# Making the operands of a two-way recurrence in the input projection, by feature block for all tokens

## The chip, the cores and the metric

One core of a Trainium2 chip runs the whole kernel. The metric is the device time of one execution in microseconds; the runs shown below are three of the kernel before the change, and one further execution was profiled.

## What is computed

A diffusion backbone of two layers works on 1024 latent tokens and 256 context tokens of width 1024. In each layer a token mixer is followed by a feed-forward part; one combined projection feeds two groups of heads, a two-way RWKV-7 recurrence (8 heads of 64, in pairs: NP = 4 blocks of 128 features) and attention with latent queries, keys and values (8 heads). Cut to the mixer's recurrence and what it reads:

```python
def rwkv_prepare(z, w0, w_b, a0, a_b, g_b, k_k, k_a):
    r, k, v, w_lo, a_lo, g_lo = jnp.split(z, idx, axis=-1)
    w_log = -softplus(-(w0 + einsum('btdl,dlc->btdc', tanh(w_lo), w_b))) - 0.5
    decay = exp(-exp(w_log))
    a = sigmoid(a0 + einsum('btdl,dlc->btdc', a_lo, a_b))
    g = sigmoid(g_lo) @ g_b
    kk = k * k_k, normalised per head
    k_dir = k[:, :, None, :] * (1.0 + (a - 1.0) * k_a)

def step(s, inp):                     # once per token and direction
    r_t, w_t, k_t, v_t, kk_t, a_t = inp
    sa = einsum('bhvk,bhk->bhv', s, kk_t)
    s = s * w_t - sa * (kk_t * a_t) + v_t k_t^T
    return s, einsum('bhvk,bhk->bhv', s, r_t)

bonus = sum(r * k_dir * r_k, over directions and features) * v
out = (group_norm(y) + bonus) * g
```

z is the projection after a filter of three taps along the tokens. Direction 1 runs through the tokens backwards. Attention (`mla_prepare`, `attend`) normalises its latents, applies the rotary tables to part of the queries and keys, and takes a softmax over all keys.

## The kernel before

Each layer goes through four stages: `in_proj`, `mixer`, `out_proj`, `ffn`. Layer 0's `in_proj` also makes the modulation of both layers from 48 chunks of `w_ada` (`modulation`). A scheduler sets a fixed order of the instructions of each engine ahead of the run; an engine works through its list in order and waits where an operand is missing. All transfers are issued by SP's queue, in order.

**Projection.** The transposed input lies in SBUF as high and low halves (`uh`, `ul`). A column j of 128 features is made by `col(j)`: `split_w` loads the weights and splits them (ACT L264, DVE L266), `project` issues 72 matmuls (L280) for all 1280 tokens, or 48 for the 1024 latents, into one of two PSUM buffers `pj`. `conv` applies the filter (ACT L287, DVE L291 and L294). Small results (sums of squares, means) use two PSUM buffers `sm`; temporaries of 128x1280 have nine buffers. First come the attention's latents, keys and values, then `queries` (the six weights of `w_uq`, rotary products L419 to L424, writes L411 and L426 into `qD`) behind the first key column. The columns follow in this order:

```python
            order = (4, 5, 6, 7, 12, 13, 8, 9, 10, 11, 0, 1, 2, 3, 14)
```

Keys are 4 to 7 (normalised to kk, ss L480), the LoRA inputs 12 and 13, values 8 to 11 (centred per head, mu L469), r 0 to 3, gate 14 (`gates`). r, k, v, kk and centred v are written to DRAM (`rkvD`), the LoRA inputs to `loD`, the gate's product to `gD`.

**Mixer.** It has ten iterations of 128 tokens per direction; direction 0 goes forwards and direction 1 backwards, so iteration i takes two different token groups (`groups`). `mixer` interleaves attention blocks with the two 64-token steps of the recurrence:

```python
            for i in range(10):
                ...
                self.rwkv_seq(l, i, 0)
                self.rwkv_seq(l, i, 1)
                if i < 9:
                    self.rwkv_inv2(l, i + 1)
                ...
                if i < 8:
                    self.rwkv_prep(l, i + 2)
```

`rwkv_prep` loads r, k, v, kk (L668) and the LoRA inputs, makes the LoRA products (L647, tanh L651), the running sums of the decay (scans L676 and L678), their exponentials E and En (L682, L684), and on POOL the products kd, ta, BK and KR (L687 to L713). It transposes v (L721) and copies it into W (L724). Then g = KR against BK (L736), its masks (L739, L742), and the transposes of BK (L746). `rwkv_bonus` (L586 to L600) makes the bonus where the second direction reaches a token group. `rwkv_inv` solves the 64-token block by 62 steps on DVE (L789, L790). `rwkv_seq` (L841 to L890) carries the state. `attn` has scores L939, maximum L940, exponential L952, transposes L971, copies L974 and L976, values L981. `rwkv_out` applies norm, bonus and gate.

Of the kernel before, what the change touches and what calls it, by code (L numbers as in the profile page):

```python
# [19 lines left out]
D = 1024  # L20
# [40 lines left out]
CO_RST = 486  # L61
CO_N = 998


N_EARLY = 7

# [13 lines left out]
class Kern:  # L80
# [8 lines left out]
    def run(self):  # L89
        tc, nc, a = self.tc, self.nc, self.a  # L90
        with ExitStack() as st:
            dp = st.enter_context(tc.tile_pool(name="dram", bufs=1, space=DRAM))
            cp = st.enter_context(tc.tile_pool(name="const", bufs=1, reuse_waits="tile"))
            self.cst = cp.tile([128, CO_RST], F32, name="cst")
            nc.sync.dma_start(out=self.cst, in_=a["consts"][:, 0:CO_RST])
# [5 lines left out]
            self.rkvD = [dp.tile([20, 128, NTOK], F32, name=f"rkvD{l}") for l in range(DEPTH)]  # L101
            self.loD = [dp.tile([3, 128, NTOK], F32, name=f"loD{l}") for l in range(DEPTH)]
# [5 lines left out]
            self.kdD = [dp.tile([NTOK // 128, 128, NP, 128], F32, name=f"kdD{l}") for l in range(DEPTH)]  # L108
            self.gD = [dp.tile([NP, 128, NTOK], F32, name=f"gD{l}") for l in range(DEPTH)]
            self.boD = [dp.tile([NTOK // 64, 128, NP, 64], F32, name=f"boD{l}") for l in range(DEPTH)]  # L110
            self.mixD = [dp.tile([NTOK // 128, 128, 8, 128], F32, name=f"mixD{l}") for l in range(DEPTH)]
            self.pv, self.msc = [], []
# [114 lines left out]
    def first_u(self, p, pp, pj):  # L227
# [3 lines left out]
        def tile(name, n):  # L231
            return p.tile([128, NTOK], F32, name=name, tag="t", bufs=9)[:, :n]

        def load(t):
# [4 lines left out]

        k4 = lambda t: t[:, :1024].rearrange("p (k n) -> p k n", k=4)  # L240
        spare = [lambda tag=f"{nm}{i}": k4(p.tile([128, NTOK], F32R, name="wt", tag=tag).bitcast(F32))
                 for i in range(3) for nm in ("lh", "ll")]
        spare += 5 * [self.mod_tile] + 5 * [lambda: k4(tile("wt", NTOK))]
# [52 lines left out]
    def in_proj(self, l, up):  # L296
# [3 lines left out]
        with ExitStack() as st:  # L300
            wp = st.enter_context(tc.tile_pool(name=f"iw{l}", bufs=3, side="right", reuse_waits="tile"))
            p = st.enter_context(tc.tile_pool(name=f"ip{l}", bufs=1, reuse_waits="tile"))
# [3 lines left out]
            if l == 0:  # L306
                self.alloc_u(up)
                self.mod_setup(st, 2, sm)
                self.first_u(p, sm, pj)
                todo = [(0, ch) for ch in range(8, 24)] + [(1, ch) for ch in range(24)]  # L310
# [91 lines left out]
            def queries():  # L402
# [24 lines left out]

            def gates(o, n):

                nc.scalar.activation(o[:, :n], o[:, :n], AF.Tanh, scale=0.5)  # L430
                nc.gpsimd.tensor_scalar(o[:, :n], o[:, :n], 0.5, 0.5, op0=ALU.mult, op1=ALU.add)
                h, lo = tmp("gh", F32R), tmp("gl", F32R)
                nc.scalar.activation(h[:, :n], o[:, :n], AF.Copy)
                nc.vector.tensor_tensor(lo[:, :n], o[:, :n], h[:, :n], op=ALU.subtract)
                w = self.split_w(a["g_b"][l], 512, wp)
                parts = [[[x[:, so:so + sn] for so, sn in SEGS]] for x in (h, lo)]
                for q in range(NP):
                    ps = pj.tile([128, 1536], F32, name="pj", tag="pj")
                    wq = [[x[:, q * 128:(q + 1) * 128] for x in w[0]]]
                    self.project(ps, wq, *parts, range(3 if need_ctx else 2))  # L440
                    g = tmp("g")
                    nc.scalar.activation(g[:, :n], ps[:, :n], AF.Copy)
                    nc.sync.dma_start(out=self.gD[l][q, :, :n], in_=g[:, :n])


            order = (4, 5, 6, 7, 12, 13, 8, 9, 10, 11, 0, 1, 2, 3, 14)
            for i, j in enumerate(order):
                full = need_ctx or 4 <= j < 14
                n = NTOK if full else NLAT
                ps = col(j, (0, 1, 2) if full else (0, 1))  # L450
                if i == 0:
                    queries()
                for m in todo[len(todo) * i // 15:len(todo) * (i + 1) // 15]:
                    self.modulation(*m)
                o = tmp("o")
                self.conv(o, ps, PV_CONV + 3 * j, pv, full)
                if j == 14:
                    gates(o, n)
                    continue
                if j >= 12:  # L460
                    nc.sync.dma_start(out=self.loD[l][j - 12], in_=o)
                    continue
                nc.sync.dma_start(out=self.rkvD[l][j, :, :n], in_=o[:, :n])
                if j >= 8:

                    oc = tmp("oc")
                    for so, sn in SEGS:
                        mu = sm.tile([128, 512], F32, name="mu", tag="sm")
                        nc.tensor.matmul(mu[:, :sn], self.cst[:, CO_BLK:CO_BLK + 128], o[:, so:so + sn], start=True, stop=True)  # L469
                        nc.vector.scalar_tensor_tensor(oc[:, so:so + sn], mu[:, :sn], -1.0 / 64, o[:, so:so + sn],  # L470
                                                       op0=ALU.mult, op1=ALU.add)
                    nc.sync.dma_start(out=self.rkvD[l][16 + j - 8], in_=oc)
                if 4 <= j < 8:
                    kcol = pv[:, PV_KK + j - 4:PV_KK + j - 3]
                    sq = tmp("sq")
                    nc.scalar.activation(sq, o, AF.Square, scale=kcol)
                    rn = tmp("rn")
                    for so, sn in SEGS:
                        ss = sm.tile([128, 512], F32, name="ss", tag="sm")
                        nc.tensor.matmul(ss[:, :sn], self.cst[:, CO_BLK:CO_BLK + 128], sq[:, so:so + sn], start=True, stop=True)  # L480
                        nc.vector.tensor_scalar(rn[:, so:so + sn], ss[:, :sn], 1e-24, None, op0=ALU.max)
                    nc.scalar.activation(rn, rn, AF.Ln)
                    nc.scalar.activation(rn, rn, AF.Exp, scale=-0.5)
                    nc.vector.scalar_tensor_tensor(rn, o, kcol, rn, op0=ALU.mult, op1=ALU.mult)
                    nc.sync.dma_start(out=self.rkvD[l][12 + j - 4], in_=rn)
# [57 lines left out]
    def rwkv_setup(self, l, st):  # L543
        tc, nc, a = self.tc, self.nc, self.a
# [4 lines left out]
        p = R.pr  # L549
        R.rst = p.tile([128, 512], F32, name="rst")  # L550
        nc.sync.dma_start(out=R.rst, in_=a["consts"][:, CO_RST:CO_N])
        R.eps = R.p.tile([128, 1], F32, name="eps")
        nc.gpsimd.memset(R.eps, GN_EPS)
        R.wb = p.tile([128, 512], F32, name="wb")
        nc.sync.dma_start(out=R.wb, in_=a["w_b"][l])
        R.ab = p.tile([128, 512], F32, name="ab")
        nc.sync.dma_start(out=R.ab, in_=a["a_b"][l])

        R.hb = p.tile([128, 16], F32, name="hb")
        nc.vector.tensor_scalar(R.hb, self.pv[l][:, PV_W0:PV_W0 + 16], 0.5, None, op0=ALU.mult)  # L560
        R.ka = p.tile([128, 8], F32, name="ka")
# [64 lines left out]
    def rwkv_prep(self, l, i):  # L626
# [33 lines left out]
        for d, tg in enumerate(self.groups(i)):  # L660
# [3 lines left out]
            for nm, j in (("r", 0), ("k", 4), ("v", 16), ("kk", 12)):  # L664
                if nm == "r" and not out_y:
                    continue
# [656 lines left out]
```

## Time and profile before

| | us |
|---|---|
| median of three runs (lowest, highest) | 4727.77 (4719.02, 4730.01) |
| the profiled execution: time, span | 4722.71, 4720.9 |
| busy PE, DVE, ACT, POOL in the span | 4203.5, 2814.2, 1779.0, 1081.6 |
| layer 0: projection, mixer, output, feed-forward | 573, 902, 131, 954 |
| layer 1: the same | 416, 874, 143, 727 |

The engines are PE (matmul), PEld (its weight loads), DVE (vector), ACT (scalar), POOL (GpSimd) and SP (whose queue issues the transfers). The first part of the profile gives each engine's busy time in the span; the stages in the last two lines are cut from the trace where one stage's matmuls follow another's. The mean granted clock of PE over the span was 0.922. The profile's wait view names, for each wait, the instruction whose end released it; its groups by line give busy time, the mean of one instruction, and the idle time ahead of them.

### The profile page before, as it was taken

The numbers are of one execution on the slowest core, as the hardware profiler recorded it, in microseconds if no ns is written. First come the engines' busy times: TensorE is split into PE (matmuls) and PEld (weight loads), VectorE is DVE, ScalarE is ACT, GpSimd is POOL, SyncE is SP. The second block draws the span as 40 slices with busy tenths as digits, with TensorE's granted clock in tenths as the row PEclk, the third lists the DMA queues.
The fourth block names the chain that finished last, engine by engine and source line by source line (L and its number), as shares of the span: only waits on it lengthen the run. The fifth ranks groups of instructions, "written<-read, shape, count | busy, mean of one in ns | idle before, by whom it ended". The sixth has DMA issues, their size and how long they took to land. (4 is left out here: it accounts for less than half of the span.)

```text
span 4720.9 us, 73923 instructions
## 1 busy us (share of the span) xinstructions
PE 4203.5 (89%) x29722; PEld 3387.0 (72%) x29722; DVE 2814.2 (60%) x4905; ACT 1779.0 (38%) x3484; POOL 1081.6 (23%) x1126
## 2 busy tenths in 40 slices
PE   8979988887888899999998989788888768999998
PEld 6757666666666788888886868566666656888887
DVE  3233378788885644444546243578888857555556
ACT  3221265554554432222224231555555634222222
POOL 1000054444442400000004000334454434100002
PEclk9999988788888999999998999878888979999999
DMA  4246722222223311111113232311222233211111
GB/s 169 99 151 218 237 65 71 57 70 66 70 64 119 110 45 34 41 39 34 47 34 107 81 106 109 91 47 51 61 69 68 60 118 133 67 50 45 45 52 65
DMA packets 305063, 385.13 MB, mean 82 GB/s; under 512 B 59088, under 2 KB 208016, under 8 KB 304720
## 3 DMA queue, kind: packets, MB, share of 16 engines
q1 hardware_dynamic: 304720, 380.41, 25.5%
q8 instruction: 233, 3.82, 0.3%
q14 instruction: 110, 0.90, 0.1%
HBM read 287.95 MB, written 92.37 MB: 81 GB/s over the span
## 5 line engine op out<-in xcount | busy, mean ns | idle before, releaser
L1133 PE MATMUL up<-u,hi 128*128 128x512 f32 (+1 forms) x3520 | 1012.2, 369 | 2.9 <-ACT hi L1124 2.9
L1133 PEld LDWEIGHTS up<-u,hi 128*128 128x128 f32 x3520 | 643.4, 189 | 118.1 <-ACT hi L1124 3.1
L1133 PE MATMUL up<-u,lo 128*128 128x512 f32 (+1 forms) x1760 | 648.3, 368 | 0.1
L280 PE MATMUL pj<-u,whi 128*128 128x512 f32 (+1 forms) x1888 | 544.4, 374 | 44.7 <-DVE o L294 33.9
L1180 DVE TENSOR_TENSOR acc<-dn,acc 128x512 f32<-128x512 f32 x340 | 233.5, 689 | 432.2 <-PE dn L1174 432.1
L280 PEld LDWEIGHTS pj<-u,whi 128*128 128x128 f32 x1888 | 342.3, 192 | 124.8 <-issue 53.4
L1133 PEld LDWEIGHTS up<-u,lo 128*128 128x128 f32 x1760 | 332.2, 189 | 58.3 <-DVE lo L1126 0.5
L939 PE MATMUL sp<-ka,qa 96*128 96x512 f32 (+1 forms) x1200 | 340.1, 417 | 36.0 <-ACT P L952 33.7
L981 PE MATMUL av<-pT,va 128*64 128x128 f32 x2624 | 253.8, 319 | 120.1 <-DVE pT L976 75.6
L280 PE MATMUL pj<-u,wlo 128*128 128x512 f32 (+1 forms) x944 | 351.8, 373 | 0.0
L1124 ACT ACTIVATE hi<-raw 128x512 fp32r<-128x512 f32 x176 | 110.5, 630 | 566.1 <-PE up L1133 563.1
L1174 PE MATMUL dn<-hi,fh 128*128 128x512 f32 x792 | 311.6, 393 | 8.4 <-DVE acc L1180 4.3
L1174 PE MATMUL dn<-lo,fh 128*128 128x512 f32 x792 | 310.0, 391 | 0.0
L1174 PE MATMUL dn<-hi,fl 128*128 128x512 f32 x792 | 305.9, 390 | 0.0
L981 PEld LDWEIGHTS av<-pT,va 128*64 128x64 f32 x2624 | 163.4, 156 | 190.3 <-DVE pT L976 74.6
L789 DVE TENSOR_TENSOR tmp<-Dt,T 128x126 f32<-128x126 f32 (+22 forms) x620 | 292.6, 472 | 11.6
L939 PEld LDWEIGHTS sp<-ka,qa 96*128 96x128 f32 x1200 | 228.7, 217 | 85.2 <-ACT P L952 42.9
L952 ACT ACTIVATE P<-sp,mx 128x512 f32<-128x512 f32 (+1 forms) x400 | 240.2, 609 | 125.6 <-DVE mx L949 75.2
L790 DVE TENSOR_TENSOR T<-T,tmp 128x126 f32<-128x126 f32 (+22 forms) x620 | 272.4, 439 | 12.0
L264 ACT ACTIVATE whi<-raw 128x512 fp32r<-128x512 f32 (+2 forms) x110 | 66.0, 603 | 545.6 <-PE pj L280 480.9
L940 DVE TENSOR_REDUCE mx<-sp 128x1 f32<-128x512 f32 (+1 forms) x400 | 229.3, 587 | 70.6 <-PE sp L939 68.8
L971 PE MATMUL tp<-cst,P 128*128 128x128 f32 x1312 | 252.7, 320 | 11.2 <-ACT P L952 9.1
(257 smaller groups left out, 7797.0 us busy)
## 6 DMA issues: line engine op xcount, KB each, us to landing
wt<-in_w_ada_dram SPq DMA_DIRECT2D x96, 512.0 KB
raw<-in_w_up_dram SPq DMA_DIRECT2D x176, 256.0 KB
raw<-in_w_down_dram SPq DMA_DIRECT2D x88, 256.0 KB
raw<-in_w_in_dram SPq DMA_DIRECT2D x84, 256.0 KB
rkvD<-o SPq DMA_DIRECT2D x20, 640.0 KB
k<-rkvD SPq DMA_DIRECT2D x40, 256.0 KB
v<-rkvD SPq DMA_DIRECT2D x40, 256.0 KB
kk<-rkvD SPq DMA_DIRECT2D x40, 256.0 KB
```

What stands on the lines that cost most here:

```text
L280: nc.tensor.matmul(ps[:, o:o + n], ww, u[k][s], start=k == 0 and j == 0, stop=k == nk - 1 and j == 2)
L789: eng.tensor_tensor(tv, bc(Dt[:, j + 1:, j:j + 1], [128, r, w]), bc(T[:, j:j + 1, :w], [128, r, w]), op=ALU.mult)
L790: eng.tensor_tensor(T[:, j + 1:, :w], T[:, j + 1:, :w], tv, op=ALU.subtract)
L939: nc.tensor.matmul(sp[:, o - b0:o - b0 + n], q[:, qq, e], A.k[e][:, kk, o:o + n], start=m == 0, stop=m == 2)
L940: nc.vector.tensor_reduce(mx[:, i:i + 1], sp[:, :w], axis=AX.X, op=ALU.min)
L952: nc.scalar.activation(P[:, o:o + w], sp[:, :w], AF.Exp, bias=mn, scale=-1.0, accum_out=mx[:, 4 + i:5 + i])
L971: nc.tensor.transpose(tp[:, b, e], Ps[e][:, o:o + 128], self.ident)
L981: nc.tensor.matmul(av[half[e], 0:128], A.v[:, k0 // 128 + kt, half[e]], pT[:, b, e], start=kt == 0, stop=kt == nkt - 1)
L1124: nc.scalar.activation(hi, raw, AF.Copy)
L1133: nc.tensor.matmul(ps[:, so:so + sn], ww, uu[k][s], start=k == 0 and m == 0, stop=k == 7 and m == 2)
L1174: nc.tensor.matmul(ps, x[:, t * 128:(t + 1) * 128], w, start=m == 0, stop=m == 3 * len(js) - 1)
L1180: nc.vector.tensor_tensor(dst, ps, dst, op=ALU.add)
```

## The change

Making the recurrence's operands moves from `rwkv_prep` to `in_proj`. The LoRA columns 12 and 13 come first and stay in SBUF. Then, for each block q of 128 features and all 1280 tokens: the key column, the value column (with 2 x 10 transposes), the r column, the LoRA products, scans, exponentials, products, and the bonus. The products are on DVE, where most were on POOL. Results go to DRAM, in the direction's own order of tokens, as `vtD`, `kkD`, `bkD` and `boD`; the decay over 64 tokens stays in SBUF (`pc`). The gate column follows, and then, in a new pool of buffers, the attention's latents, keys, values and last its queries. Temporaries have 13 buffers. `rwkv_prep` now loads BK, KR and W, with two buffers for BK, and goes on with g. PE has 22422 instructions for 22484, DVE 4941 for 4907, ACT 2574 for 3086, POOL 539 for 1131, SP 1808 for 1420.

```diff
+                def lora(w, x, bcol, q):
+                    ts = [tmp("lt") for d in range(2)]
+                    for so, sn in SEGS:
+                        ps = [sm.tile([128, 512], F32, name="lo", tag="sm") for d in range(2)]
+                        for d in range(2):
+                            nc.tensor.matmul(ps[d][:, :sn], w[half[d], q * 128:(q + 1) * 128], x[half[d], so:so + sn],
+                                             start=True, stop=True)
+                        for d in range(2):
...
+                            nc.scalar.activation(dst, src[:, ::-1] if d else src, AF.Tanh, bias=hb[:, b:b + 1], scale=0.5)
+                    return ts
...
+                for q in range(NP):
+                    k, kk = key(q)
+                    v = value(q)
+                    r = column(q, need_ctx)
+                    ths, tas = lora(wb, lw, 0, q), lora(ab, la, 8, q)
+                    kds = []
+                    for d in range(2):
+                        th, ta = ths[d], tas[d]
+                        rv = (lambda t: t[:, ::-1]) if d else (lambda t: t)
+                        nc.scalar.activation(th, th, AF.Copy, scale=0.5, bias=0.5)
+                        Ls = tmp("Ls")
+                        for t in (0, NTOK // 2):
+                            nc.vector.tensor_tensor_scan(Ls[:, t:t + NTOK // 2], rst, th[:, t:t + NTOK // 2], 0.0,
+                                                         op0=ALU.mult, op1=ALU.add)
...
+                        nc.scalar.activation(E[:, :, 1:65], chunks(Ls), AF.Exp, scale=-C0)
+                        nc.scalar.activation(Ls, Ls, AF.Exp, scale=C0)
...
+                        nc.vector.tensor_tensor(chunks(o), chunks(rv(kk)), E[:, :, 0:64], op=ALU.mult)
+                        nc.sync.dma_start(out=self.kkD[l][d, 0, q], in_=o)
...
+                        nc.vector.tensor_tensor(chunks(o), chunks(r), Er[:, :nr // 64], op=ALU.mult)
+                        nc.sync.dma_start(out=self.kkD[l][d, 1, q, :, :nr], in_=o)
+                        kd = tmp("kd")
+                        nc.scalar.activation(kd, ta, AF.Identity, scale=ka[:, q:q + 1], bias=ka[:, 4 + q:5 + q])
+                        nc.vector.tensor_tensor(kd, kd, rv(k), op=ALU.mult)
+                        kds.append(kd)
+                        nc.vector.scalar_tensor_tensor(ta, ta, 1.0, rv(kk), op0=ALU.add, op1=ALU.mult)
+                        nc.vector.scalar_tensor_tensor(ta, ta, 0.5, Ls, op0=ALU.mult, op1=ALU.mult)
+                        nc.sync.dma_start(out=self.bkD[l][d, 1, q], in_=ta)
+                        nc.vector.tensor_tensor(Ls, kd, Ls, op=ALU.mult)
+                        nc.sync.dma_start(out=self.bkD[l][d, 0, q], in_=Ls)
+                    kb = tmp("kb")[:, :nr]
+                    nc.vector.tensor_tensor(kb, kds[0][:, :nr], kds[1][:, ::-1][:, :nr], op=ALU.add)
+                    nc.vector.scalar_tensor_tensor(kb, kb, pv[:, PV_RK + q:PV_RK + q + 1], r, op0=ALU.mult, op1=ALU.mult)
+                    bo = tmp("bo")
+                    for so, sn in SEGS[:3 if need_ctx else 2]:
+                        ps = sm.tile([128, 512], F32, name="bop", tag="sm")
+                        nc.tensor.matmul(ps[:, :sn], self.cst[:, CO_BLK:CO_BLK + 128], kb[:, so:so + sn], start=True, stop=True)
+                        nc.vector.tensor_tensor(bo[:, so:so + sn], ps[:, :sn], v[:, so:so + sn], op=ALU.mult)
...
+                o = column(14, need_ctx)
+                gates(o, nr)
...
-            for nm, j in (("r", 0), ("k", 4), ("v", 16), ("kk", 12)):
...
-            nc.scalar.activation(th, th, AF.Copy, scale=0.5, bias=0.5)
...
-                eng.tensor_tensor(BK[he, :, :, kt], self.rev(kd[he], d), nE, op=ALU.mult)
-                eng.tensor_tensor(BK[he, :, :, bt], self.rev(ta[he], d), nE, op=ALU.mult)
...
+            for e in range(2):
                 he = half[e]
...
+                for kind, o in ((0, 64 * (1 - e)), (1, 64 * e)):
+                    for c in range(2):
+                        src = self.bkD[l][d, kind, :, he, s * 128 + c * 64:s * 128 + c * 64 + 64]
+                        nc.sync.dma_start(out=BK[he, :, c, o:o + 64], in_=src.rearrange("q p t -> p q t"))
+                nc.sync.dma_start(out=KR[he, e].rearrange("p q c t -> p q (c t)"),
+                                  in_=self.kkD[l][d, 0, :, he, tok].rearrange("q p t -> p q t"))
             if out_y:
...
+                    nc.sync.dma_start(out=KR[:, 2, :, c], in_=self.kkD[l][d, 1, :, :, b * 64:b * 64 + 64].rearrange("q p t -> p q t"))
...
+                    nc.sync.dma_start(out=Ws[c][half[1 - e], e, d], in_=self.vtD[l][d, s, half[c], :, e * 64:e * 64 + 64])
```

The order in which the scheduler puts this stands below at three places; lines are those of the changed kernel.

PE in the projection of layer 0, from the end of the second block's r column (pj, L282) on; lo is a LoRA product, bop the bonus, ps and pt a modulation chunk:

```order
L282 MATMUL pj<-u_115,wlo 128x256
L384 MATMUL lo<-lw,wb 128x512
L384 MATMUL lo<-lw,wb 128x256 x2
L384 MATMUL lo<-la,ab 128x512 x4
L384 MATMUL lo<-la,ab 128x256 x2
L477 MATMUL bop<-kb,cst 128x512 x2
L477 MATMUL bop<-kb,cst 128x256
L173 MATMUL ps<-wt,sc 32x256 x8
L188 MATMUL pt<-cst,ev 128x2 x2
```

Of the twelve LoRA matmuls nine stand in one piece behind the r column; three are spread over its last 33 rows, with 31 projection matmuls between the first LoRA matmul and the bonus. In layer 1 there are 72.

DVE in the first block of layer 0, from the second key product on; lt is the second LoRA's result, kb the bonus operand that bop above reads:

```order
L465 SCALAR_TENSOR_TENSOR lt<-lt,rn 128x1280
L455 TENSOR_TENSOR kx<-rn,E 128x1280
L459 TENSOR_TENSOR rx<-o,E 128x1280
L466 SCALAR_TENSOR_TENSOR lt<-lt,Ls 128x1280
L463 TENSOR_TENSOR kd<-kd,o 128x1280
L465 SCALAR_TENSOR_TENSOR lt<-lt,rn 128x1280
L468 TENSOR_TENSOR Ls<-kd,Ls 128x1280
L472 TENSOR_TENSOR kb<-kd 128x1280
L466 SCALAR_TENSOR_TENSOR lt<-lt,Ls 128x1280
L473 SCALAR_TENSOR_TENSOR kb<-kb,pv_93,o 128x1280
L468 TENSOR_TENSOR Ls<-kd,Ls 128x1280
L478 TENSOR_TENSOR bo<-bop,o 128x512
```

kb (L473) stands behind all products of both directions but one. Ahead of these rows on DVE stand four scans (L443) and the first direction's kx, rx and kd of this block.

SP at the start of layer 0's mixer; qD are the queries (the last two rows of it the rotary parts, L600), BK and KR the first operands of g:

```order
L585 DMA qD_75<-tm 2x64x1280 x4
L729 DMA BK<-bkD_69 64x4x64
L591 DMA cosT<-in_rope_dram 128x1024
L592 DMA sinT<-in_rope_dram 128x1024
L729 DMA BK<-bkD_69 64x4x64 x15
L600 DMA qD_75<-tm 8x16x1280 x2
L730 DMA KR<-kkD_71 64x4x128 x2
L735 DMA KR<-kkD_71 128x4x64 x2
L738 DMA W<-vtD_73 64x4x64 x4
L730 DMA KR<-kkD_71 64x4x128 x2
L735 DMA KR<-kkD_71 128x4x64 x2
```

The rotary writes now stand ahead of the first KR load. Before the change they stood in the projection, behind the first key column.

## Rows read from the trace of the kernel before

**Rows 1.** Stage windows: length, busy PE, PEld, DVE, ACT, POOL; PEclk, DMA share, GB/s

```profile
573.00:1475.00 902.00, 747.15 (x8298) 584.12 (x8296) 723.07 (x1590) 504.53 (x1229) 395.82 (x458) 0.84 0.25 71
...
2560.00:2976.00 416.00, 377.74 (x1777) 305.41 (x1775) 142.60 (x179) 110.45 (x135) 19.47 (x18) 0.95 0.29 98
2976.00:3850.00 874.00, 701.96 (x7879) 549.58 (x7879) 695.34 (x1515) 478.85 (x1164) 372.25 (x431) 0.84 0.23 63
```

**Rows 2.** Waits of PE in mixer 0: us in total, times, longest

```profile
PE av L981 <- DVE pT L976: 37.0, 22, 6.1
```

**Rows 3.** Groups by line, mixer 0 (573:1475): busy us, mean ns, idle before

```profile
L789 DVE TENSOR_TENSOR tmp<-Dt,T 128x126 f32<-128x126 f32 (+22 forms) x310 | 146.3, 472 | 6.0
L790 DVE TENSOR_TENSOR T<-T,tmp 128x126 f32<-128x126 f32 (+22 forms) x310 | 137.0, 442 | 6.2
...
L706 POOL TENSOR_TENSOR BK<-kd,En 64x512 f32<-64x512 f32 x40 | 51.4, 1285 | 46.5 <-PE bt L746 44.9
...
L591 DVE SCALAR_TENSOR_TENSOR kb<-kb,pv,r 128x128 f32<-128x128 f32 x40 | 23.6, 640 | 0.0
L647 PE MATMUL lo<-LZ,wb 128*128 128x256 f32 x80 | 23.4, 423 | 1.7 <-ACT sq L616 1.2 <-ACT LZ L639 0.5
...
L651 ACT ACTIVATE ta<-lo,hb 128x128 f32<-128x128 f32 x80 | 23.1, 392 | 0.0
...
L594 PE MATMUL bo<-kb,cst 128*128 128x512 f32 x20 | 13.8, 779 | 10.9 <-DVE kb L591 6.2 <-DVE mx L949 4.8
...
L678 DVE TENSOR_TENSOR_SCAN Ls<-rst,th 128x512 f32<-128x512 f32 x10 | 12.6, 1259 | 0.0
...
L721 PE MATMUL vt<-cst,vr 128*128 128x128 f32 x40 | 8.1, 339 | 0.2 <-ACT AB L743 0.2
```

**Rows 4.** Timeline, mixer 0, DVE and POOL: start us, us, engine, line

```profile
722.62 1.30 DVE L789 TENSOR_TENSOR tmp<-Dt,T 128x120 f32<-128x120 f32 x1
...
721.10 2.67 POOL L706 TENSOR_TENSOR BK<-kd,En 64x512 f32<-64x512 f32 x2
...
732.08 0.27 DVE L789 TENSOR_TENSOR tmp<-Dt,T 128x136 f32<-128x136 f32 x1
```

**Rows 5.** Groups by line and shape, projection of layer 1 (2560:2976): the same columns

```profile
L287 ACT ACTIVATE o<-pj,pv 128x1280 f32<-128x1280 f32 x10 | 13.1, 1314 | 0.0
...
L469 PE MATMUL mu<-o,cst 128*128 128x512 f32 x16 | 7.5, 592 | 0.0
...
L484 DVE SCALAR_TENSOR_TENSOR rn<-o,pv,rn 128x1280 f32<-128x1280 f32 x4 | 6.2, 1552 | 12.1 <-ACT rn L483 12.1
L361 DVE TENSOR_TENSOR tm<-pj,rb 128x1280 f32<-128x1280 f32 x4 | 6.0, 1492 | 9.5 <-PE pj L280 9.5
```

**Rows 6.** The queries: timeline of layer 1, window, waits of PE (layers 1, 0)

```profile
2741.57 0.40 PE L280 MATMUL pj<-ll,whi 128*128 128x512 f32 x1
2741.81 0.39 PE L280 MATMUL pj<-lh,wlo 128*128 128x512 f32 x1
...
2763.07 2.34 POOL L419 TENSOR_TENSOR t<-tm,sinT 128x1024 f32<-128x1024 f32 x1 [62.96 <-DMA sinT<-in_rope_dram]
...
2772.99 1.02 SPq L426 DMA_DIRECT2D qD<-tm  x1
...
2770.00:2776.00 6.00, 4.02 (x10) 3.20 (x11) 4.26 (x5) 3.61 (x4) 0.36 (x1) 0.54 0.43 109
...
PE pj L280 <- DVE o L294: 14.1, 1, 14.1
...
PE pj L280 <- ACT gh L433: 7.2, 1, 7.2
...
PE pj L280 <- DVE o L294: 19.8, 1, 19.8
```

**Rows 7.** Timeline of SP's queue at the start of mixer 0

```profile
575.74 2.29 SPq L636 DMA_DIRECT2D LZ<-loD  x2
578.08 0.59 SPq L668 DMA_DIRECT2D r<-rkvD  x1
```

More of the change, by code (lines that the diff above doesn't have):

```diff
@@ L60 @@
 CO_H0 = 483
-CO_RST = 486
-CO_N = 998
+CO_N = 486
 N_EARLY = 7
+TW = NTOK + NTOK // 64
+NT = 13
 class Ctx:
@@ L237, in load @@
             return x
[L240 to L243, printed above, removed]
+        k4 = lambda t: t.rearrange("p (k n) -> p k n", k=4)
+        spare = 5 * [self.mod_tile] + 11 * [lambda: k4(tile("wt", 1024))]
         xt = []
@@ L446, in in_proj @@
[L446 to L485, printed above, removed]
@@ L568, in rwkv_setup @@
         R.X = [R.p.tile([128, 16, 64], F32, name=f"X{i}") for i in range(2)]
-        R.LZ = [p.tile([128, 2, 256], F32, name=f"LZ{i}") for i in range(2)]
         for i in range(2):
             nc.gpsimd.memset(R.X[i], 0.0)
-            nc.gpsimd.memset(R.LZ[i], 0.0)
     def groups(self, i):
@@ L632, in rwkv_prep @@
         half = [slice(0, 64), slice(64, 128)]
-        lz = R.LZ[i % 2]
+        Ws = [R.p.tile([128, 2, 2, NP, 64], F32, name="W", tag="W", bufs=4) for c in range(2)]
+        KRs, GAs, BTs = [], [[], []], [[], []]
         for d, tg in enumerate(self.groups(i)):
-            dst = lz[half[d], :, d * 128:(d + 1) * 128]
-            nc.sync.dma_start(out=dst, in_=self.loD[l][0:2, half[d], tg * 128:(tg + 1) * 128].rearrange("x p t -> p x t"))
-        for d in range(2):
-            t = lz[half[d], 0, d * 128:(d + 1) * 128]
-            nc.scalar.activation(t, t, AF.Tanh)
@@ L641, in lora @@
-        def lora(w, x, bcol, tag):
-            ts = [p.tile([128, NP, 128], F32, name=tag, tag=f"{tag}{d}") for d in range(2)]
-            for q2 in range(2):
-                ps = pp.tile([128, 2, 2, 128], F32, name="lo", tag="r")
-                for j in range(2):
-                    q = 2 * q2 + j
-                    nc.tensor.matmul(ps[:, j], w[:, q * 128:(q + 1) * 128], lz[:, x], start=True, stop=True)
-                for j in range(2):
-                    for d in range(2):
-                        b = bcol + 4 * d + 2 * q2 + j
-                        nc.scalar.activation(ts[d][:, 2 * q2 + j], ps[:, j, d], AF.Tanh, bias=R.hb[:, b:b + 1], scale=0.5)
-            return ts
@@ L722, in rwkv_prep @@
+            if out_y:
+                for c in range(2):
+                    b = 2 * tg + (1 - c if d else c)
+                    nc.sync.dma_start(out=KR[:, 2, :, c], in_=self.kkD[l][d, 1, :, :, b * 64:b * 64 + 64].rearrange("q p t -> p q t"))
             for c in range(2):
                 for e in range(2):
-                    nc.scalar.activation(Ws[c][half[1 - e], e, d], vt[half[c], :, e], AF.Copy)
+                    nc.sync.dma_start(out=Ws[c][half[1 - e], e, d], in_=self.vtD[l][d, s, half[c], :, e * 64:e * 64 + 64])
```

258 lines of the change are left out of this document (127 added, 131 removed).

## The prediction

> **What bounds the kernel now.** I read the stage windows first. In the first layer's mixer (573 to 1475 us) PE is busy 747.15 of 902 us, VectorE (DVE) 723.07, and in the second's (2976 to 3850 us) 701.96 and 695.34 of 874, at a granted clock of 0.84 in both [rows 1]. So two engines are nearly full there, and each waits for the other. In the projection of layer 1 (2560 to 2976 us) PE is busy 377.74 of 416 us at 0.95, while DVE (142.60), ACT (110.45) and POOL (19.47) stand mostly idle [rows 1]. That is what the change uses: operand making leaves the stage in which everything is busy. The waits of PE in the mixer come next: the largest, 37.0 us in 22 pieces, is attention's product with the values, waiting for DVE's copy of the transposed softmax [rows 2]. It is not for an operand of the recurrence. What moves out frees engines; it does not end this wait by itself.
>
> The profiled execution took 4722.7 us, 5 us below the median of the runs shown; the sum is made against it. About 0.3% (14 us) is what a measurement of this kernel can tell from no change.
>
> **What leaves the mixers.** From the groups by line of mixer 0 [rows 3]:
> - PE: the LoRA matmuls 23.4 us for one of two weights, so about 45, the value transposes 16 (the row is the reversed half, 8.1), the bonus 13.8: 75 us. For layer 1, which makes a little less, I take 73.
> - DVE: the bonus products 23.6, scans 12.6 and as much for the other direction, bonus times value about 7: 55 us.
> - POOL: the two lines of BK products 51.4 each; the others, by the same 1.28 us for 512 columns, four lines of 20 products, two of 10, and 80 quarter products: some 265 of the 396 us in rows 1.
> - ACT: 160 tanh at 0.39 us, 80 copies into W of the same price, 100 exponentials and copies of 512 columns at some 0.6: about 150 us of 505.
>
> POOL's share matters to DVE. In the timeline a recurrence step on DVE takes 1.30 us while POOL multiplies beside it, and 0.27 us ten microseconds later with POOL idle [rows 4]. The 620 such steps of a mixer cost 146.3 + 137.0 us [rows 3]; at 0.27 each they would cost 167, so overlap costs up to 116. With 265 of 396 us of POOL gone I take two thirds, 78 us. DVE in mixer 0 falls to about 723 - 55 - 78 = 590 us.
>
> What that is worth: PE's work is then 747 - 75 = 672 and 702 - 73 = 629 us. PE's idle time is 155 us in mixer 0 and 172 in mixer 1. At the top it all stays (nothing shortens the chain of scores, softmax, transposes and values, whose last link rows 2 show), at the bottom nearly all goes and the clock rises too (rivals). I take half, because DVE's load falls by a fifth while its dependence chain stays: 672 + 78 = 750 (-152) and 629 + 86 = 715 (-159). **Mixers: -311 us.**
>
> **What the projections gain.** Per block of 128 features the order on PE is now: key and value column, 20 transposes, r column, 12 LoRA matmuls, then 2 or 3 bonus matmuls. These read kb, which DVE finishes only after its whole list for the block. PE works in order, so it stands still at the bonus until then. Between the first LoRA matmul and the bonus lie only 31 projection matmuls in layer 0 (mostly of 256 columns) and 72 in layer 1. By the prices of a column of 72 of them, which start 0.24 us apart at 512 columns [rows 6], these are 6 and 14 us.
> - The chain: six tanh of 512 or 256 columns (0.39 us per 128 columns [rows 3] bounds them from above), the second LoRA's six, a copy of 1280 columns at about 1.3 us [rows 5] and the first exponential of the same size: 10 to 13 us until DVE runs freely.
> - DVE, 128x1280 each: a scan over 512 takes 1.26 us [rows 3], so over 640 about 1.55, four of them 6.1; nine plain products or sums at 1.49 [rows 5] 13.4; five with a scalar at 1.55 [rows 5] 7.7, less one product that follows kb, plus two weight splits between: 27 us.
> - Together 40 us. Layer 0: 40 - 6 = 34 us of standstill, the 20 transposes 4 (half of the 8.1 us of rows 3), the bonus 2.3 (a matmul of 512 columns in full precision has two records, 7.5 us for 16 [rows 5]), and 2 us for the half-rate restart that rows 6 show after a standstill (granted clock 0.54 for 6 us): 42. Layer 1: 26 + 4 + 2 + 2.5, and 3.5 for the r column, which waits on the key's filter: 38.
> - The last block has no columns left beside its LoRA matmuls: 48 in each layer.
>
> That is 3 x 42 + 48 + 3 x 38 + 48 = 336 us. Bounds: if DVE and ACT ran the list twice as fast the blocks would cost about 190, if none of the 31 and 72 matmuls helped, 416. I stay with the durations of the rows. The gate column already made PE wait 7.2 us for its split [rows 6]; now the new pool of the queries stands behind it and must wait for the old one's last buffers. I take as much again: 7 us per layer, 14 in all.
>
> **The queries are moved to the end.** Their rotary chain cost a standstill already: the last query matmul at 2741.81, POOL's first product only at 2763.07 when the tables have come, the last write of queries issued at 2772.99 [rows 6]. So 31 us after PE's last matmul the queries are complete; columns stood behind it then, and PE still waited 19.8 and 14.1 us in one piece [rows 6]. Now the mixer's first matmuls stand there. SP's queue has the rotary writes ahead of the first KR load, and those wait on DVE. Hence g comes after the chain: 31 us in layer 1, six more in layer 0 by its longer wait, 5 each for the restart at half rate, together 78; less the old waits of 34, and less 9 that I assume the mixer's first loads took in any case: +35 over both. **Projections with boundary: +385 us.**
>
> **The loads.** Each iteration of a mixer now issues 32 loads of 64 KB or so where it issued 10. SP takes 0.6 us for a load of r, and 1.15 us each for the LoRA pieces with two regions [rows 7]; at 0.6 that is 19 us of a 75 us iteration. I cost it at nothing, since loads are issued an iteration ahead and the queue has free time; the price when that cover is gone is under the rivals. The Trainium skill ("DMA: Bandwidth & Descriptors", section "Rules for kernel authors") speaks against this part: many small transfers should be coalesced, because under 64 KB one pays mostly overhead. No run here shows such loads yet; by that rule the fifth case below would deserve more than its chance.
>
> **Sum:** 4722.7 + 385 - 311 = 4797 us.
>
> **Rivals.**
> 1. *The mixers gain far more (the other side).* Both partners of the PE-DVE exchange lose work at once, and POOL's interference with it. If three quarters of PE's idle time go and the clock rises from 0.84 to 0.90, the mixers take 672 x 0.84/0.90 + 39 = 666 and 587 + 43 = 630: -480 us, so 4628. For it: the steps of 1.30 against 0.27 [rows 4], and a PE that stands still less is granted the full clock more. Against: the largest waits are the softmax's [rows 2]. It decides faster from a gain of 399 us in the mixers, 200 each.
> 2. *The mixers lose only PE's moved work.* Idle time stays: -148, so 4960. For it: the softmax chain has the same length. Against: DVE was 80% busy.
> 3. *The wait at the bonus is short,* so that the change does to the projections what it says: DVE's list would have to end with the LoRA matmuls. With a chain of 22 us for 40 the blocks cost 8 x 18 = 144 less: 4653. Against: the printed order of both engines, and the durations of rows 5.
> 4. *The loads become the bound.* If SP's 14 us more per iteration stand in the path in 20 iterations: +280, some 5080. For it: SP also waits in order for attention results. Against: DMA share 0.25 in the mixer [rows 1].
>
> **How the numbers follow.** Forecast 0.50, rivals 0.26, 0.13, 0.06, 0.05. The forecast's own range is 4740 to 4860, of which 0.03 lies on the faster side, 0.06 within 0.3%, 0.41 slower. Rival 1 gives 0.25 faster, 0.01 same; rival 3 0.06 faster; rivals 2 and 4 0.18 slower. So faster 0.34, same 0.07, slower 0.59. The range reaches from 4620, the middle of rival 1, to 4930, short of rival 2: some 0.1 on each side lies outside.
>
> **What would show it.** In the projections: a wait of PE at the bonus matmul for DVE's kb, eight times, 26 to 40 us each; a projection longer by 190 us (layer 1 by somewhat less). At the boundary: the first g matmul waiting for a KR load issued behind the rotary writes. In the mixers: POOL at about 130 us, DVE near 590, recurrence steps at 0.3 to 0.35 us in the mean, length near 750 and 715 us. The prediction is wrong if the eight waits are below 15 us, if the mixers fall below 680, or if they stay above 800.

## The result

The changed kernel takes 4783.17 us (median of four runs, 4780.08 to 4793.09), the kernel before in its runs beside it 4723.4 us. The ratio is 1.0141, with a 95% interval from 1.0099 to 1.0182: slower by some 60 us. The forecast was 4797 us. The profiled execution of the changed kernel has a span of 4782.8 us, 61.9 us more than that of the kernel before.

The stage windows of the changed kernel, with the columns of [rows 1], are cut at the last projection matmul, at the mixer's first g matmul, and at the first matmul of the output stage:

```profile
0.00:743.00 743.00, 597.75 (x3235) 430.60 (x3236) 295.25 (x412) 227.62 (x297) 34.08 (x41) 0.88 0.43 150
743.00:793.00 50.00, 0.55 (x6) 0.38 (x4) 7.27 (x7) 0.00 (x0) 8.50 (x8) 0.53 0.38 112
793.00:1559.00 766.00, 663.46 (x8037) 518.05 (x8038) 581.13 (x1521) 368.30 (x864) 124.23 (x135) 0.87 0.29 75
...
2637.00:3200.00 563.00, 451.62 (x1959) 337.03 (x1958) 235.03 (x253) 201.71 (x249) 33.43 (x29) 0.86 0.27 92
3200.00:3244.00 44.00, 0.84 (x4) 0.38 (x4) 7.00 (x7) 0.00 (x0) 8.49 (x8) 0.54 0.37 110
3244.00:3922.00 678.00, 604.48 (x7633) 477.04 (x7633) 553.50 (x1456) 341.04 (x799) 111.08 (x121) 0.90 0.30 75
```

Cut the same way, the kernel before has its projection of layer 0 up to 573, that of layer 1 over 406 us from its first matmul, and mixers of 910 and 890 us. The window of layer 1's projection above begins 9.5 us ahead of its first matmul; from that matmul on it takes 554 us. So the projections grew by 170 and 148 us, a stretch of 50 and 44 us with a nearly idle PE stands at each boundary, and the mixers are 144 and 212 us shorter. That sums to +56; the rest lies in the other stages.

Of what the projections grew by, only about half is waiting. This is the row of layer 0's projection before; layer 1's is in [rows 1]:

```profile
0.00:573.00 573.00, 508.43 (x3039) 388.63 (x3040) 195.98 (x333) 135.64 (x184) 27.87 (x26) 0.96 0.50 172
```

PE is busy 89 us longer in layer 0 (508 to 598) and 74 us longer in layer 1 (378 to 452), by the matmuls that moved in and at a granted clock of 0.88 and 0.86 for 0.96 and 0.95; its idle time accounts for the rest.

The waits of PE in the changed kernel, whole span (us, times, longest), where [rows 2] and the waits of [rows 6] stood before:

```profile
PE bop L477 <- DVE kb L473: 146.8, 8, 19.7
PE g L750 <- DMA KR<-kkD: 57.5, 5, 49.4
PE g L750 <- DMA W<-vtD: 43.2, 1, 43.2
PE av L983 <- DVE pT L978: 38.4, 42, 3.3
```

The eight waits at the bonus of the projection and the two long ones at the first g are new. The third row is the boundary of layer 1, where the last load to come is a W; it stands in the queue behind the rotary writes as the KR loads do. The wait for attention's softmax copy, 37.0 us in mixer 0 and 75.6 in both mixers before, is 38.4 in both now.

The second block of layer 0 in the timeline (start us, us), first PE, then DVE:

```profile
298.40 1.12 PE L384 MATMUL lo<-lw,wb 64*128 64x512 f32 x2
...
316.41 1.22 PE L384 MATMUL lo<-la,ab 64*128 64x256 f32 x2 [1.54 <-ACT lt L390]
335.91 4.41 PE L477 MATMUL bop<-kb,cst 128*128 128x512 f32 x6 [18.29 <-DVE kb L473]
```

```profile
310.09 2.87 DVE L443 TENSOR_TENSOR_SCAN Ls<-rst,lt 128x640 f32<-128x640 f32 x2 [2.15 <-ACT lt L440]
314.58 1.51 DVE L455 TENSOR_TENSOR kx<-rn,E 128x1280 f32<-128x1280 f32 x1 [1.61 <-ACT E L447]
...
334.23 1.54 DVE L473 SCALAR_TENSOR_TENSOR kb<-kb,pv,o 128x1280 f32<-128x1280 f32 x1
```

From the first LoRA matmul to the bonus pass 37.5 us: 11.7 until DVE scans, 25.7 for its list. Of these 38 us PE is busy 16, at a mean granted clock of 0.69 (1.00 in the first 8 us, in which the 31 projection matmuls run, 0.78 in the 11 us of the last LoRA matmuls, and 0.50 in the standstill):

```profile
298.00:336.00 38.00, 16.23 (x61) 8.64 (x59) 25.84 (x21) 19.19 (x23) 3.30 (x4) 0.69 0.32 127
```

DVE's recurrence steps took 0.472 and 0.442 us each before in mixer 0 [rows 3]; over both mixers they are now:

```profile
L792 DVE TENSOR_TENSOR T<-T,tmp 128x126 f32<-128x126 f32 (+22 forms) x620 | 191.2, 308 | 11.0
L791 DVE TENSOR_TENSOR tmp<-Dt,T 128x126 f32<-128x126 f32 (+22 forms) x620 | 189.4, 306 | 11.2
```

SP's queue at the boundary of layer 0 (start us, us for the issues of the group):

```profile
734.59 8.22 SPq L585 DMA_DIRECT2D qD<-tm  x1
742.91 12.04 SPq L729 DMA_DIRECT2D BK<-bkD  x1
755.02 2.82 SPq L591 DMA_DIRECT2D cosT<-in_rope_dram  x1
757.93 1.46 SPq L592 DMA_DIRECT2D sinT<-in_rope_dram  x1
...
780.14 4.08 SPq L600 DMA_DIRECT2D qD<-tm  x2
786.81 1.58 SPq L730 DMA_DIRECT2D KR<-kkD  x2
```

A single load of BK holds the queue for 12.04 us, right behind the query writes (16.66 us at the same place in layer 1). The rotary tables are issued only after it, the rotary products then run on POOL and DVE from 774 to 784 us, their writes go out, and after these the first KR load.

### The profile page after: what moved, and what is told of

Its sections match the earlier page's. It is cut to its first block, busy times and chain, and to the rows that moved or that the text cites. A ratio compares the mean times of both kernels' runs of the same rounds, so it can differ in the third digit from the quotient of the medians.

```text
span 4782.8 us, 72976 instructions
## 1 busy us (share of the span) xinstructions
PE 4192.3 (88%) x29598; PEld 3324.7 (70%) x29598; DVE 2733.8 (57%) x4939; ACT 1680.7 (35%) x2972; POOL 586.0 (12%) x534
## 5 line engine op out<-in xcount | busy, mean ns | idle before, releaser
L282 PE MATMUL pj<-u,whi 128*128 128x512 f32 (+1 forms) x1888 | 562.0, 382 | 13.9 <-DVE o L296 9.3
L282 PEld LDWEIGHTS pj<-u,whi 128*128 128x128 f32 x1888 | 348.3, 195 | 114.5 <-issue 43.4
L282 PE MATMUL pj<-u,wlo 128*128 128x512 f32 (+1 forms) x944 | 355.6, 377 | 0.0
L941 PE MATMUL sp<-ka,qa 96*128 96x512 f32 (+1 forms) x1200 | 330.1, 405 | 28.4 <-ACT P L954 21.7
L983 PE MATMUL av<-pT,va 128*64 128x128 f32 x2624 | 238.7, 306 | 61.7 <-DVE pT L978 38.4
L941 PEld LDWEIGHTS sp<-ka,qa 96*128 96x128 f32 x1200 | 217.2, 208 | 77.7 <-ACT P L954 29.8
L750 PE MATMUL g<-KR,BK 64*128 64x128 f32 (+1 forms) x1280 | 173.2, 323 | 108.8 <-DMA KR<-kkD 57.5
L268 DVE TENSOR_TENSOR wlo<-raw,whi 128x512 fp32r<-128x512 f32 (+2 forms) x110 | 71.8, 655 | 311.2 <-ACT whi L266 288.2
L973 PE MATMUL tp<-cst,P 128*128 128x128 f32 x1312 | 240.9, 307 | 9.7 <-ACT P L954 9.0
L750 PEld LDWEIGHTS g<-KR,BK 64*128 64x128 f32 x1280 | 149.7, 222 | 129.9 <-issue 115.0
```

The source lines that it names most:

```text
L268: nc.vector.tensor_tensor(lo[:, :m], raw[:, :m], hi[:, :m], op=ALU.subtract)
L282: nc.tensor.matmul(ps[:, o:o + n], ww, u[k][s], start=k == 0 and j == 0, stop=k == nk - 1 and j == 2)
L750: nc.tensor.matmul(g[:, q] if out_y else g[:, q, 0], BK[he, q, c, :], rhs, start=True, stop=True)
L941: nc.tensor.matmul(sp[:, o - b0:o - b0 + n], q[:, qq, e], A.k[e][:, kk, o:o + n], start=m == 0, stop=m == 2)
L973: nc.tensor.transpose(tp[:, b, e], Ps[e][:, o:o + 128], self.ident)
L983: nc.tensor.matmul(av[half[e], 0:128], A.v[:, k0 // 128 + kt, half[e]], pT[:, b, e], start=kt == 0, stop=kt == nkt - 1)
```

## The experiments

Each is compared with the kernel before on its own chip (its medians there were 4717.6, 4718.9 and 4718.7 us), and read against the changed kernel's 4783. The changed kernel was not run again beside them, and the kernel before moved by 6 us between its sessions, so a difference of that size tells nothing.

**Queries ahead of keys and values.** In the last part of `in_proj`:

```diff
+            ch, cl, rs = latent((15, 16, 17), PV_QN, segs, nq)
...
             ch, cl, rs = latent((18, 19), PV_KVN, (0, 1, 2), NTOK)
...
-            ch, cl, rs = latent((15, 16, 17), PV_QN, segs, nq)
...
```

> The changed kernel, with the queries made ahead of the attention's keys and values in the last part of the projection. My theory: the 49 and 44 us in which PE stands before the mixer's first g matmul are the queries' rotary chain and the slow query writes ahead of the KR loads in the queue; behind other matmuls they are hidden, the two waits together fall from 93 to under 30 us, and the time from 4783 to about 4715 (4700 to 4735). Rival: the first operands' loads take that long whatever stands ahead of them; the waits stay above 60 us and the time within 20 us of 4783.

Measured: 4740.96 us, ratio 1.0046 (1.0026 to 1.0065), 42 us less. The first g now follows the last projection matmul by 10 and 7 us, as the theory had it, but the time misses its range (4700 to 4735) by 6 us, because the projections became 25 and 33 us longer. Its waits show where:

```profile
PE pj L282 <- ACT whi L266: 24.0, 5, 9.7
PE pj L282 <- DVE wlo L268: 22.9, 2, 11.5
```

The weights of the following matmuls come late, because their loads now stand behind the query writes:

```profile
642.17 4.17 SPq L553 DMA_DIRECT2D qD<-tm  x1
646.44 11.12 SPq L264 DMA_DIRECT2D raw<-in_w_in_dram  x1
```

So the queue itself is held, whatever stands behind it. The 76 us won at the boundaries and the 58 lost in the projections leave 18. The largest other part is mixer 0, with the same code: 728 us at a granted clock of 0.91, for 766 at 0.87. The theory had not named that part, and no run here says why the clock differs.

**The bonus operand first.** In the block's loop:

```diff
-                    ths, tas = lora(wb, lw, 0, q), lora(ab, la, 8, q)
+                    tas = lora(ab, la, 8, q)
                     kds = []
+                    for d in range(2):
...
+                        kd = tmp("kd")
...
+                    nc.vector.scalar_tensor_tensor(kb, kb, pv[:, PV_RK + q:PV_RK + q + 1], r, op0=ALU.mult, op1=ALU.mult)
+                    ths = lora(wb, lw, 0, q)
+                    bo = tmp("bo")
...
                     for d in range(2):
                         th, ta = ths[d], tas[d]
```

> The changed kernel, with the second LoRA product, kd of both directions, kb and the bonus ahead of the scans, exponentials and products. My theory: the eight PE waits at the bonus (147 us) are DVE's list ahead of kb; with four operations ahead of it, kb is ready some 17 us after the first LoRA matmul where it took 31 to 45, the waits fall to under 50 us and the time by 90 to 140 us, to about 4670. Rival: DVE's and ACT's whole list per block is the bound, and PE then waits at the next columns' filters instead: the time falls by less than 30 us.

Measured: 4776.94 us, ratio 1.0126 (1.0103 to 1.0149), 6 us less, which is no clear difference. The wait at the bonus is gone (6.8 us in all of layer 0), but the projections are only 8 and 6 us shorter. Waits of PE in the whole span that stand there instead:

```profile
PE pj L282 <- DVE o L296: 61.5, 3, 20.5
...
PE pt L188 <- DVE ev L175: 30.9, 12, 5.8
...
PE pt L182 <- DVE ev L175: 27.5, 9, 5.6
PE pj L282 <- ACT gh L330: 26.6, 2, 22.8
```

In layer 1 PE stands still at the first projection matmul behind the bonus, up to 20.5 us, for a filter (L296); in layer 0 it waits for the copies of the modulation chunks. Both stand behind the block's list on DVE, as here in layer 1 (DVE's last rows of a list, then PE):

```profile
2852.56 1.48 DVE L481 TENSOR_TENSOR Ls<-kd,Ls 128x1280 f32<-128x1280 f32 x1
2853.95 1.27 DVE L296 SCALAR_TENSOR_TENSOR o<-pj,pv,o 128x1023 f32<-128x1023 f32 x1
```

```profile
2856.28 1.19 PE L282 MATMUL pj<-u,whi 128*128 128x512 f32 x2 [20.49 <-DVE o L296]
```

The rival holds: the list per block is what PE waits for, and the bonus was only the first place where it did.

**Query writes by head.**

```diff
-                        nc.sync.dma_start(out=qd[2 * j:2 * j + 2, 0:64, :nq], in_=t[:, :nq])
+                        for e in range(2):
+                            nc.sync.dma_start(out=qd[2 * j + e, 0:64, :nq], in_=t[64 * e:64 * e + 64, :nq])
...
-                    nc.sync.dma_start(out=qd[:, 64 + 16 * i:80 + 16 * i, :nq], in_=o[:, :nq])
+                    for e in range(H):
+                        nc.sync.dma_start(out=qd[e, 64 + 16 * i:80 + 16 * i, :nq], in_=o[16 * e:16 * e + 16, :nq])
```

> The changed kernel, with each write of queries split into one per head (8 for 4, and 16 for 2). My theory: the four writes with two heads in the outer dimension move at 45 to 60 GB/s and hold the queue, so the rotary tables and the first loads come late; by head they move several times faster, the first-g waits fall from 93 us to 45 to 65, the time by 25 to 50 us, to about 4745. Rival: the rotary products on DVE and POOL and the loads themselves set the wait; the time changes by less than 15 us.

Measured: 4738.45 us, ratio 1.0046 (1.0026 to 1.0066), 45 us less. The boundaries shrink from 50 and 44 to 20 us each. The transfers' rate in 40 equal slices of 728 to 770 us, first in the changed kernel, then in this one:

```profile
GB/s 59 49 66 49 54 54 49 59 49 59 49 59 49 49 59 49 59 49 59 49 54 54 49 59 49 59 103 59 49 220 336 205 324 107 59 49 111 51 54 150
```

```profile
GB/s 288 24 0 132 180 276 44 0 132 180 284 155 236 375 362 150 162 82 42 94 113 87 106 63 151 166 176 181 176 171 171 156 143 195 214 159 87 157 177 218
```

With two heads in the outer dimension the writes move at 49 to 66 GB/s for 27 us on end; by head they come and go at up to 288, and the load of BK behind them takes 0.88 us to issue, for 12.04. In the changed kernel's stretch the busy share of the core's 16 DMA engines is 0.13, about two of the sixteen (the column behind the clock):

```profile
730.00:756.00 26.00, 13.54 (x72) 11.36 (x70) 4.47 (x3) 0.00 (x0) 1.02 (x3) 0.81 0.13 54
```

The Trainium skill ("DMA: Bandwidth & Descriptors", section "Why a DMA increments its semaphore by 16 and not by 1") says that the slowest dimension larger than one sets how many DMA engines a transfer gets: two for these writes, all sixteen for 64 rows. The share of 0.13 and the two rows of rates agree.

**All three.**

> The three edits together. If they are two separate losses, the gains of the first two add up and the third gives little more: 4783 - 65 - 110 = about 4605 (4570 to 4650), under the kernel before. If the bound only shifts from one place to the next, it stays above 4680.

Measured: 4642.79 us, ratio 0.9841 (0.9821 to 0.986): 140 us under the changed kernel and 1.6% under the kernel before. That lies in the range given (4570 to 4650), but the sum behind it does not hold: alone the three edits gained 42, 6 and 45 us, 93 together. The first g follows the projection by 10 and 7 us, and the projections are no longer than in the changed kernel (690 and 552 us from first to last matmul, for 700 and 554). By the traces 76 us of the gain lie at the boundaries, 12 in the projections, and 49 and 9 in the two mixers, whose code is unchanged and whose granted clock is 0.92 for 0.87 and 0.90:

```profile
743.20:1460.30 717.10, 623.68 (x7997) 486.85 (x7997) 573.56 (x1502) 362.30 (x843) 119.47 (x131) 0.92 0.32 81
...
3109.30:3778.50 669.20, 583.85 (x7584) 458.62 (x7584) 544.08 (x1433) 334.29 (x776) 106.42 (x117) 0.92 0.31 78
```

**First and third edit alone.**

> The changed kernel with the queries ahead of keys and values and their writes by head, without the second edit. It tells what the second edit is worth in the fourth experiment (4643 us), where it was worth only 6 us alone. Theory: DVE's list per block sets the pace of the projection, so the second edit is worth little here too: 4645 to 4665. Rival: it is worth its expected size once the writes no longer hold the queue: 4700 or more.

Measured: 4683.06 us, ratio 0.9923 (0.9897 to 0.9948), between the two expectations. The second edit is thus worth 40 us in the fourth experiment. By the traces the projections have 18 of it, mixer 0 some 22, and there the code is the same: with the edit it took 717 us at a granted clock of 0.92 (above), without it 739 at 0.89:

```profile
751.00:1490.20 739.20, 638.65 (x7996) 499.39 (x7996) 571.16 (x1502) 360.14 (x843) 119.38 (x131) 0.89 0.31 77
```

Why that mixer's clock differs stays open.

**Queries last in the kernel before.**

```diff
-                if i == 0:
-                    queries()
...
+            queries()
```

> The kernel before, with the queries alone moved from behind the first key column to the end of the projection. My theory: this move by itself costs what the changed kernel pays at the boundary, 93 us of waits for the first g less the 34 us of standstill that the early place had: 40 to 70 us, so about 4775. Rival: in the kernel before, other work of the mixer's start covers the rotary chain; within 20 us of 4718.

Measured: 4763.52 us, ratio 1.0098 (1.0076 to 1.012), 45 us more, as the theory had it. The move by itself costs as much as three quarters of the 60 us by which the changed kernel is slower. PE waits in front of the LoRA matmuls that began the mixer then, for the rotary products and for the LoRA inputs (LZ), whose loads stand behind the query writes:

```profile
PE lo L646 <- POOL t L419: 33.2, 1, 33.2
...
PE lo L646 <- ACT LZ L638: 28.7, 1, 28.7
```

**Writes by head in the kernel before.** The third edit, on the kernel before.

> The kernel before, with the query writes split by head as in the third experiment. My theory: the old standstill of 20 and 14 us behind the queries was the same slow writes; most of it goes, the time falls by 20 to 40 us to about 4690. Rival: the filter that PE waited for stands behind the rotary products on DVE, whatever the writes do; within 15 us of 4718.

Measured: 4685.38 us, ratio 0.9926 (0.9907 to 0.9945), 34 us less, and the two old waits of 19.8 and 14.1 us [rows 6] are gone. So the slow writes were a fault of both kernels. With this edit in both, 4738 stands against 4685: the change still costs 53 us. With the queries also ahead of keys and values and the bonus operand first, the change's layout reaches 4643 and is ahead by 43.

**POOL's work put back.** In `rwkv_prep`, for each direction:

```diff
+            for _ in range(10):
+                nc.gpsimd.tensor_tensor(R.z[2], R.z[0], R.z[1], op=ALU.mult)
```

> The changed kernel, with 200 products of 128x512 on scratch tiles put back on POOL in each mixer (256 us each, as much as moved out), read by nobody. My theory: a good part of the mixers' gain is DVE freed of this interference; the 62-step recurrence goes from 0.31 to 0.42 to 0.47 us a step, and each mixer becomes 30 to 70 us longer: about 4880. Rival: the gain is PE's and DVE's moved instructions; the steps slow down but the time rises by less than 30 us.

Measured: 4970.79 us, ratio 1.0536 (1.0521 to 1.0552), 188 us more. Mixer 0 is 69 us longer and mixer 1 107, at the upper end of what was expected and above it; the rest is small. DVE's steps are where they were before the change:

```profile
L743 POOL TENSOR_TENSOR z<-z,z 128x512 f32<-128x512 f32 x400 | 515.2, 1288 | 25.0
...
L796 DVE TENSOR_TENSOR tmp<-Dt,T 128x126 f32<-128x126 f32 (+22 forms) x620 | 294.8, 476 | 10.8
L797 DVE TENSOR_TENSOR T<-T,tmp 128x126 f32<-128x126 f32 (+22 forms) x620 | 286.3, 462 | 11.2
```

In the mixers (cut as before) DVE is busy 96 and 106 us longer, and PE is idle 44 and 81 us longer:

```profile
797.90:1632.40 834.50, 687.82 (x8037) 535.28 (x8037) 677.33 (x1521) 369.48 (x863) 361.66 (x323) 0.83 0.27 69
...
3324.10:4109.10 785.00, 630.62 (x7632) 493.30 (x7632) 659.17 (x1457) 341.43 (x799) 351.05 (x311) 0.85 0.26 66
```

Work that nobody reads, on an engine that has time for it, takes back half of the 356 us that the mixers gained. These products wait for nothing, so they may delay POOL's own few steps more than the old ones did; the share is an upper bound for that reason.

**The loads twice.** Each operand load is issued again, into a scratch tile:

```diff
-                        nc.sync.dma_start(out=BK[he, :, c, o:o + 64], in_=src.rearrange("q p t -> p q t"))
+                        for T in (BK, zB):
+                            nc.sync.dma_start(out=T[he, :, c, o:o + 64], in_=src.rearrange("q p t -> p q t"))
```

> The changed kernel, with each of the mixer's operand loads issued a second time into scratch tiles that nobody reads (64 for 32 in an iteration). My theory: the loads are covered; beyond the start of each mixer, where the queue is in the path, nothing changes: 4783 to 4810. Rival: SP's queue is near its limit; each iteration grows by the 15 us or so of 32 more issues, in all 150 us or more: above 4900.

Measured: 4839.41 us, ratio 1.0253 (1.0232 to 1.0274), 56 us more, between the two. The waits of g for a KR load grew from five to thirteen:

```profile
PE g L757 <- DMA KR<-kkD: 149.1, 13, 53.8
```

Two of the thirteen, 53.8 and 45.7 us, are the boundaries; the eleven inside the mixers sum to 50 us, where four summed to 8. At 32 loads an iteration they are covered but for the start of each mixer; at 64 they are not, though far from the 150 us of a queue that sets the pace. By stage, mixer 1 has 48 of the 56 us. Whether the issues or the doubled transfers cost this was not separated.

**The next key column ahead of a block's operands**, on the kernel of all three edits, with 14 buffers:

```diff
...
+                ahead = key(0)
+                for q in range(NP):
+                    now = ahead + (value(q), column(q, need_ctx))
+                    if q < NP - 1:
+                        ahead = key(q + 1)
+                    operands(q, *now)
```

> The fourth experiment's kernel, with the key column of the next block ahead of a block's operand making (14 buffers for temporaries). Theory: what is left in the projection is PE standing behind DVE's list of a block, and the 14 us of a column's matmuls hide part of it: 8 to 15 us less in seven blocks, 4540 to 4590. Rival: the columns' filters stand behind the list on DVE, so the standstill only moves again: within 20 us of 4643.

Measured: 4686.23 us, ratio 0.9924 (0.9898 to 0.9949), 43 us more than all three edits, outside both expectations. The rival's mechanism holds and costs more than its 20 us: PE waits for the value column's filter at the mean's matmul,

```profile
PE mu L414 <- DVE o L296: 82.1, 6, 19.7
```

because that filter stands behind the list on DVE.

**All columns of the next block ahead**, on the kernel of the first and third edit, with 14 buffers:

```diff
...
+                ahead = columns(0)
+                for q in range(NP):
+                    now = ahead
+                    if q < NP - 1:
+                        ahead = columns(q + 1)
+                    else:
+                        gates(column(14, need_ctx), nr)
+                    operands(q, *now)
```

> The ninth experiment's kernel, with all three columns of the next block, and the gate column, ahead of a block's operand making (14 buffers for temporaries). Theory: 40 us of matmuls stand between a block's values and its bonus, the whole chain is covered: 100 to 150 us under the ninth. Rival: 14 buffers are too few, DVE's list stands ahead of the next filters, and PE waits for released buffers instead: less than 40 us under it.

Measured: 4706.08 us, ratio 0.9971 (0.9958 to 0.9985), 23 us more than without. The wait at the bonus did not go, it grew:

```profile
PE bop L477 <- DVE kb L473: 189.1, 8, 27.3
```

In three of the four blocks of each layer the scheduler set the LoRA matmuls behind the new columns as well, so no more projection matmuls stand between them and the bonus than before. In the last block 162 and 120 do, and PE still waits 13.5 and 17.9 us. DVE's list itself became longer: in the second block it stands 4.6 us for buffers whose results are still being written out and 3.2 us for ACT, so the rival's buffers have a part in it. Whether a written-out order of PE and DVE would hide the list was not tried.

## Why the prediction was right

The forecast's case is the one that came, with its two large terms. That the total is only 14 us off is in part luck: the mixers gained 45 us more than forecast, the boundaries cost 25 us more. One sign that it had named as proving it wrong, mixers below 680 us, came true for mixer 1 by 2 us (678), though not for mixer 0 (766).

- **Mixers, -311 us forecast, -356 measured.** Forecast were 750 and 715 us, measured 766 and 678. DVE in mixer 0 is busy 581 us where 590 was worked out, POOL 124 where 130, and a recurrence step takes 0.31 us as said. The half of PE's idle time that I took to go was close as a sum and unequal by layer: PE's idle time is 103 us in mixer 0 (78 forecast) and 74 in mixer 1 (86). PE's own work fell by 84 and 97 us, more than the 75 and 73 of the moved instructions, as the granted clock rose from 0.84 to 0.87 and 0.90, a part of the first rival. The softmax wait, which the change by itself was not to end, fell by half; it is a wait for DVE, whose load fell. The returned work on POOL puts the interference at up to half of the gain, a share of the time that the sum had not set apart.
- **Projections, +316 us forecast (336 + 14, less the old standstill of 34, which lay in them), +318 measured.** The chain of 40 us from the first LoRA matmul to the bonus is 37.5 us in three blocks of layer 0 and 45.5 in three of layer 1; the last blocks took 34.6 and 31.1.
- **What failed within it** is the step "a wait of PE at the bonus matmul for DVE's kb, eight times, 26 to 40 us each": the waits are 18 us in the mean. I let PE's part of the chain be the 31 or 72 projection matmuls alone. The twelve LoRA matmuls add to it, and some of them wait until ACT has emptied a PSUM buffer: PE is busy 16 us inside the chain where 6 stood, and 25 in layer 1 where 14 stood. The sum held because it charged the chain's whole length less the projection matmuls; whether PE stands still in the rest or runs LoRA matmuls does not change it. That is also why half of the growth is busy time. The bound of 416 us in the same step was added wrongly (its own terms give 396); nothing rests on it.
- **The boundary, +78 us, or 69 with the 9 deducted for the mixer's first loads; measured 94.** The cause was named rightly, the rotary writes ahead of the first KR load. What was missed is that the slow query writes hold the queue itself: 12.04 and 16.66 us for one load, and the rotary tables behind it. The experiments on the writes, in both kernels, show that.
- **The loads** were costed at nothing. For 32 an iteration that holds, with less in hand than I thought: doubling them costs 56 us. The Trainium skill's rule on small transfers ("DMA: Bandwidth & Descriptors", section "Rules for kernel authors"), cited against this part, speaks of transfers under 64 KB. The loads here have 64 and 128 KB, and no price of theirs shows at 32 an iteration.
- **Rival 3**, a short wait at the bonus, was brought about by the second experiment, and its price was wrong: 6 us alone and 40 beside the other two edits, not 144, because the block's list comes to bear at the next filter.

## What to carry to other kernels

Moving work from a full stage to one with idle engines pays only as far as the engines of the second stage do not wait for each other in program order: eight times PE stood some 18 us at one small matmul behind DVE's list of 26 us, and moving that matmul ahead only moved the wait. Look at what each queue holds when a step is moved to a stage's end: the slow query writes cost 34 us in the middle of the stage, and moving them to its end cost the kernel before another 45. And count an idle engine's work as a cost where it slows a busy one: POOL had time to spare, and products put back on it made the mixers 69 and 107 us longer.

## What the runs showed of the hardware

A write whose outer dimension is two moved at 49 to 66 GB/s, with 0.13 of the 16 DMA engines' time busy, and held up other loads behind it in the same queue, 11 to 17 us for a single issue; splitting six writes into 24 gained 34 us before the change and 45 after it. And 256 us of POOL products per mixer, independent of everything, raised DVE's two-operand steps from 0.31 to 0.47 us in the mean.
